# Attention: the products with the values segment by segment, both parities of heads in turn

## The chip, the cores and the metric

The kernel runs on one core of one Trainium2 chip. A core has a matrix engine (TensorE: PE in the profile, its weight loads PEld), VectorE (DVE), ScalarE (ACT), GpSimd (POOL) and SyncE (SP), which issues the transfers here. The metric is the device time of one execution in microseconds (us).

## The reference

One inference step of a two-layer streaming encoder over 1024 new frames of one stream and 64 frames of a running one, width 1024, all in float32. Layer 0 is RWKV-7 time mixing and a SwiGLU feed-forward; layer 1 is sliding-window attention over keys and values that are shared, with a learned sink per head, and another feed-forward. The part that matters here is the attention: 16 query heads of 64, four key/value heads, chunks of 64 frames; the queries of a chunk see the keys of their own chunk and of the two before it.

```python
s = jnp.einsum('bnqhgd,bnkhd->bnhgqk', qc, kb, preferred_element_type=jnp.float32) * ATTN_SCALE
s = jnp.where(valid[None, :, None, None, None, :], s, NEG_INF)
p = sink_softmax(s, sinks)              # exp(s - m) / (sum exp(s - m) + exp(sink - m))
o = jnp.einsum('bnhgqk,bnkhd->bnqhgd', p.astype(v.dtype), vb)
```

## The kernel before, in words

Activations are held with features on the partitions. The tokens are worked in two halves: A, 512 frames, and B, the other 512 and the 64 of the running stream. The dense products (line names `dp`, L433 to L435) take three matmuls for each product, of float32 values split into a high and a low part: each streams 288 columns (half B) or 512 (half A) through a full 128x128 array.

`attend` calls `chunk` 8 times for half A and 9 times for half B, so 17 chunks. A chunk is worked in two passes `m`, each with four key/value-and-group combinations in two parities `par`: heads of parity 0 lie on partitions 0 to 63 and of parity 1 on 64 to 127. One pass is, in the order of the code:

1. the scores `sc`, one matmul for each `g` and `par` (L1259): keys on 64 partitions, 64 to 192 columns;
2. maximum, exponential and sum on VectorE and ScalarE, and the scaling by the reciprocal (L1261 to L1284);
3. for each parity, transposes `pt` of the probabilities (L1290), two for each segment of keys, and a copy of each segment to `a_PT` in SBUF (L1291), the first segment's on ScalarE, the second's on VectorE;
4. the products with the values `po` (L1294): for parity 0 into partitions 0 to 63 of one PSUM tile, for parity 1 into 64 to 127, one matmul for each segment, the segments added up in PSUM;
5. one copy of the 128x256 tile into the query's place `a_q` (L1297, ScalarE).

A window of keys lies in one or two tiles of 128 values. The first two chunks have one segment (of 64 or 128 keys), the other 15 have two: 128 and 64, or, where the window begins in the middle of a tile, 128 and 128, with zeros ahead. So there are 34 passes and 128 products with the values; 30 of the passes have two segments.

Buffers: `sc` has two PSUM tiles, `pt` two, `po` one; the probabilities `a_P` and their transposes `a_PT` have two each.

What stands on each engine is not the order of the code: the framework's scheduler places instructions by priority (`prio(6)` and `prio(9)` for the two attention passes over half A and half B) and by its own timing of the engines. The feed-forward of the other half has the next priority after the attention (`prio(7)`: half B, layer 0; `prio(10)`: half A, layer 1), and its `dp` matmuls are filled in wherever the attention is not ready on TensorE. Each engine then runs its own list strictly in order.

Of the kernel before, what the change touches and what calls it, by code (L numbers as in the profile page):

```python
# [1137 lines left out]
class Attention:  # L1138
# [95 lines left out]
    def chunk(self, half, i, q):  # L1234
        nc, dn, c = self.nc, self.dn, self.c
        V, S, G = nc.vector, nc.scalar, nc.gpsimd
        ch = i if half == "A" else 8 + i


        if ch == 16:  # L1240
            key = lambda h, m: self.kS[h, m, :]
            pad, nk, seg = 0, 192, [(0, 128, self.vC), (128, 64, self.vS)]
        else:
            k0, k1 = max(0, ch - 2) * 64, ch * 64 + 64
            key = lambda h, m: self.kT[h, m, k0:k1]
            pad, nk = k0 % 128, k1 - k0
            seg = [(at - k0 + pad, min(128, k1 - at), self.v[:, at // 128, :]) for at in range(k0 - pad, k1, 128)]
        sinks = self.vec["sinks"]
        for m in range(2):
            sc = []  # L1250
            mx = self.t([128, 6, 4], "mx", 2)
            for par in range(2):
                self.n += 1
                p = self.ps.tile([128, 512], F32, name=f"sc_{self.n}", tag="rc", bufs=2)[:, :2 * nk].rearrange("p (a k) -> p a k", a=2)
                sc.append(p)
            for g in range(2):
                for par in range(2):
                    h = slice(par * 64, par * 64 + 64)
                    nc.tensor.matmul(sc[par][:, g, :], lhsT=q[h, i, 4 * m + 2 * g:4 * m + 2 * g + 2, :].rearrange("p a t -> p (a t)"), rhs=key(h, m), start=True, stop=True)  # L1259
            for par in range(2):  # L1260
                V.tensor_reduce(out=mx[:, 0, 2 * par:2 * par + 2], in_=sc[par], axis=AX.X, op=ALU.max)  # L1261
            sk = sinks[:, 4 * m:4 * m + 4]
            V.scalar_tensor_tensor(out=mx[:, 1, :], in0=mx[:, 0, :], scalar=SCALE, in1=sk, op0=ALU.mult, op1=ALU.max)
            V.tensor_scalar(out=mx[:, 2, :], in0=mx[:, 1, :], scalar1=-1.0, scalar2=None, op0=ALU.mult)
            V.tensor_tensor(out=mx[:, 3, :], in0=sk, in1=mx[:, 1, :], op=ALU.subtract)
            S.activation(mx[:, 3, :], mx[:, 3, :], AF.Exp)
            P = []
            for par in range(2):
                e = self.t([128, 2, 256], "P", 2)
                if pad:  # L1270
                    G.memset(e[:, :, 0:pad], 0.0)
                for g in range(2):
                    x = 2 * par + g
                    S.activation(e[:, g, pad:pad + nk], sc[par][:, g, :], AF.Exp, scale=SCALE, bias=mx[:, 2, x:x + 1], accum_out=mx[:, 4, x:x + 1])
                P.append(e)
            V.tensor_tensor(out=mx[:, 5, :], in0=mx[:, 4, :], in1=mx[:, 3, :], op=ALU.add)
            V.reciprocal(out=mx[:, 5, :], in_=mx[:, 5, :])
            self.n += 1
            po = self.ps.tile([128, 512], F32, name=f"po_{self.n}", tag="ry", bufs=1)[:, :256]
            for par in range(2):  # L1280
                e = P[par]
                for g in range(2):
                    x = 2 * par + g
                    V.tensor_scalar(out=e[:, g, pad:pad + nk], in0=e[:, g, pad:pad + nk], scalar1=mx[:, 5, x:x + 1], scalar2=None, op0=ALU.mult)  # L1284
                self.n += 1
                pt = self.ps.tile([128, 512], F32, name=f"pt_{self.n}", tag="rp", bufs=2).rearrange("p (s g q) -> p s g q", s=2, g=2)
                eT = self.t([128, 2, 2, 128], "PT", 2)
                for si, (at, n, vv) in enumerate(seg):
                    for g in range(2):
                        nc.tensor.transpose(pt[0:n, si, g, :], e[:, g, at:at + n], c["id"])  # L1290
                    (S.copy if si == 0 else V.tensor_copy)(eT[0:n, si], pt[0:n, si])  # L1291
                for si, (at, n, vv) in enumerate(seg):
                    col = (2 * m + par) * 64
                    nc.tensor.matmul(po[par * 64:par * 64 + 64, :], lhsT=vv[0:n, col:col + 64],  # L1294
                                     rhs=eT[0:n, si].rearrange("p g q -> p (g q)"),
                                     start=si == 0, stop=si == len(seg) - 1)
            S.copy(q[:, i, 4 * m:4 * m + 4, :], po.rearrange("p (i t) -> p i t", i=4))  # L1297
# [126 lines left out]
```

## Time and profile before

| | |
|---|---|
| median of 3 runs | 3066.93 us (3064.41 to 3069.12) |
| profiled execution | 3068.17 us, its span 3066.4 us |
| PE busy | 2881.6 us, 94% of the span |
| DVE, ACT, POOL busy | 62%, 45%, 30% |
| granted TensorE clock, mean | 0.960 |
| attention over half A | about 1456 to 1640 us of the span |
| attention over half B | about 2099 to 2360 us of the span |

In the views below each row of the timeline gives the start in us from the span's beginning, how long the row's instructions took from the first start to the last end, the engine, the line, the operation, what it writes and reads, the part of the array (rows by columns) and the shape, and how many records the row holds. A float32 matmul with `sc` or `po` leaves two records, a transpose and a `dp` matmul one. The ends of matmuls overlap with the next one's start, so the time that a row occupies TensorE is read from its start to the next row's start.

### The profile page before, as it was taken

To read this page: it belongs to the slowest core of one execution; us is meant where nothing else is said; L and a number is where in the kernel's file an instruction comes from. 1 tells how busy PE (TensorE), PEld (TensorE's weight loads), DVE (VectorE), ACT (ScalarE), POOL (GpSimd) and SP (SyncE) were. 2 spreads that over 40 slices of the span, in tenths; PEclk is the share of its full clock that TensorE was granted. 3 is DMA by queue.
4 is the path that set the end of the run, shared out by engine and by line. 5 is a ranking of instruction groups with operands and counts; after the bars stand their busy time and mean duration, and the time that the engine had idled before them with its cause. 6 is when DMAs were issued, how large, how long until landed. Compare 5 with 4: busy or idle time off the path is not lost. (4 is left out here: it accounts for less than half of the span.)

```text
span 3066.4 us, 51529 instructions
## 1 busy us (share of the span) xinstructions
PE 2881.6 (94%) x19650; PEld 2475.1 (81%) x19650; DVE 1899.9 (62%) x3964; ACT 1371.4 (45%) x2489; POOL 915.9 (30%) x785
## 2 busy tenths in 40 slices
PE   6898888987999989999999999999999999999998
PEld 5677777876777767887789999887667889899998
DVE  8887798968998993357553333665555334633334
ACT  7766665544445542244653222344553233322222
POOL 6455123323343332224211222243111222322221
PEclk9999789989899999999999999999999999999999
DMA  4645353353232225232112222222112332322222
GB/s 144 174 119 149 109 140 102 109 130 118 77 97 87 90 70 139 93 111 86 62 42 73 83 83 83 77 82 79 59 62 67 95 96 73 110 83 83 84 82 70
DMA packets 262047, 289.10 MB, mean 94 GB/s; under 512 B 125028, under 2 KB 143972, under 8 KB 261800
## 3 DMA queue, kind: packets, MB, share of 16 engines
q1 hardware_dynamic: 261800, 285.81, 31.3%
q8 instruction: 154, 2.52, 0.4%
q14 instruction: 93, 0.76, 0.1%
HBM read 243.18 MB, written 41.16 MB: 93 GB/s over the span
## 5 line engine op out<-in xcount | busy, mean ns | idle before, releaser
L433 PE MATMUL dp<-xh,wh 128*128 128x288 f32 (+2 forms) x3480 | 1181.1, 341 | 26.1 <-DVE hx L962 10.2
L434 PE MATMUL dp<-xl,wh 128*128 128x288 f32 (+2 forms) x3480 | 1175.5, 338 | 10.6 <-POOL xl L426 6.3
L435 PE MATMUL dp<-xh,wl 128*128 128x288 f32 (+2 forms) x3480 | 1172.4, 337 | 0.0
L393 ACT CAST wh<-wr 128x512 fp32r<-128x512 f32 x730 | 446.2, 619 | 823.6 <-PE dp L434 633.0
L433 PEld LDWEIGHTS dp<-xh,wh 128*128 128x128 f32 x3480 | 667.0, 192 | 100.4 <-DVE hx L962 14.7
L434 PEld LDWEIGHTS dp<-xl,wh 128*128 128x128 f32 x3480 | 668.5, 192 | 73.3 <-POOL xl L426 7.6
L435 PEld LDWEIGHTS dp<-xh,wl 128*128 128x128 f32 x3480 | 668.7, 192 | 62.0 <-issue 6.2
L394 POOL TENSOR_TENSOR wl<-wr,wh 128x512 fp32r<-128x512 f32 x243 | 339.2, 1396 | 1059.0 <-ACT wh L393 954.0
L394 DVE TENSOR_TENSOR wl<-wr,wh 128x512 fp32r<-128x512 f32 x487 | 376.3, 776 | 431.5 <-ACT wh L393 423.0
L433 PE MATMUL dp<-mh,wh 128*128 128x288 f32 (+1 forms) x808 | 254.5, 315 | 1.2 <-DVE a_xB L962 1.0
L435 PE MATMUL dp<-mh,wl 128*128 128x288 f32 (+1 forms) x808 | 254.1, 314 | 0.0
L434 PE MATMUL dp<-ml,wh 128*128 128x288 f32 (+1 forms) x808 | 253.5, 314 | 0.0
L943 DVE TENSOR_TENSOR st<-st,dp 128x288 f32<-128x288 f32 (+1 forms) x132 | 70.0, 530 | 229.0 <-PE dp L435 228.6
L962 DVE TENSOR_TENSOR a_xB<-dp,a_xB 128x288 f32<-128x288 f32 x352 | 158.1, 455 | 82.9 <-PE dp L435 82.7
L945 POOL TENSOR_TENSOR xl<-st,xh 128x288 fp32r<-128x288 f32 (+1 forms) x102 | 101.8, 998 | 330.4 <-ACT xh L944 321.6
L433 PEld LDWEIGHTS dp<-mh,wh 128*128 128x128 f32 x808 | 152.3, 189 | 10.8 <-issue 2.4
L435 PEld LDWEIGHTS dp<-mh,wl 128*128 128x128 f32 x808 | 152.3, 188 | 8.1 <-issue 1.8
L434 PEld LDWEIGHTS dp<-ml,wh 128*128 128x128 f32 x808 | 152.4, 189 | 6.6 <-issue 0.8
L190 ACT COPY r_f<-r_G 32x1024 f32<-32x1024 f32 x68 | 136.0, 1999 | 37.1 <-DVE r_f L226 25.0
L962 DVE TENSOR_TENSOR hx<-dp,hx 128x512 f32<-128x512 f32 x176 | 119.5, 684 | 44.9 <-PE dp L435 44.4
L215 DVE TENSOR_TENSOR r_f<-r_f,r_f 128x60 f32<-128x60 f32 (+5 forms) x476 | 119.2, 281 | 0.5
L944 ACT CAST xh<-st 128x288 fp32r<-128x288 f32 (+1 forms) x102 | 50.2, 492 | 136.2 <-DVE st L943 135.1
(343 smaller groups left out, 3889.3 us busy)
## 6 DMA issues: line engine op xcount, KB each, us to landing
wr<-in_ffn_in SPq DMA_DIRECT2D x352, 256.0 KB
wr<-in_ffn_out SPq DMA_DIRECT2D x176, 256.0 KB
wr<-in_rkv SPq DMA_DIRECT2D x90, 256.0 KB
wr<-in_rwo SPq DMA_DIRECT2D x32, 256.0 KB
wr<-in_wq SPq DMA_DIRECT2D x32, 256.0 KB
wr<-in_wo SPq DMA_DIRECT2D x32, 256.0 KB
r_r_s<-s_s SPq DMA_DIRECT2D x17, 256.0 KB
r_sv<-s_vt SPq DMA_DIRECT2D x17, 256.0 KB
```

The costliest lines, as they stand in the source:

```text
L190: S.copy(st[32 * q:32 * q + 32].rearrange("p (t g j) -> p t g j", g=4, j=8), src)
L215: V.tensor_tensor(out=Z[:, h, 1:3, r0:4, 0:j], in0=Z[:, h, a, r0:4, j:j + 2].rearrange("p r c -> p c r").unsqueeze(3).broadcast_to([128, 2 ...
L393: nc.scalar.copy(h, x)
L394: (nc.gpsimd if self.turn % 3 == 0 else nc.vector).tensor_tensor(out=l, in0=x, in1=h, op=ALU.subtract)
L433: self.nc.tensor.matmul(ps, lhsT=wh, rhs=xh, start=i == 0, stop=False)
L434: self.nc.tensor.matmul(ps, lhsT=wh, rhs=xl, start=False, stop=False)
L435: self.nc.tensor.matmul(ps, lhsT=wl, rhs=xh, start=False, stop=i == last)
L943: V.tensor_tensor(out=t[o], in0=t[o], in1=p, op=ALU.mult)
L944: S.copy(a.hi[:, q], t[o])
L945: G.tensor_tensor(out=a.lo[:, q], in0=t[o], in1=a.hi[:, q], op=ALU.subtract)
L962: V.tensor_tensor(out=self.x[m][:, q], in0=p, in1=self.x[m][:, q], op=ALU.add)
```

## The change

The products with the values of a pass are taken out of the loop over the parities. The loop now makes the transposes and copies of both parities and keeps the two `a_PT` tiles in a list; then a loop over the segments multiplies, for each segment, parity 0 and parity 1 one after the other. The matmuls, their operands and their number are the same, and so are the copies, the buffers and the sums: each half of the tile still adds its first and then its second segment.

```diff
             po = self.ps.tile([128, 512], F32, name=f"po_{self.n}", tag="ry", bufs=1)[:, :256]
+            eTs = []
             for par in range(2):
                 e = P[par]
...
                     (S.copy if si == 0 else V.tensor_copy)(eT[0:n, si], pt[0:n, si])
-                for si, (at, n, vv) in enumerate(seg):
+                eTs.append(eT)
+
+            for si, (at, n, vv) in enumerate(seg):
+                for par, eT in enumerate(eTs):
                     col = (2 * m + par) * 64
                     nc.tensor.matmul(po[par * 64:par * 64 + 64, :], lhsT=vv[0:n, col:col + 64],
```

The scheduler makes new lists from it. The lines of `chunk` behind the change are one to four higher: L1290 becomes L1291, L1291 L1292, L1294 L1298. On TensorE, in a pass over half A with two segments of 128 keys (`pt` the transposes of one parity, `po` the products with the values, `sc` the scores of a later pass, `dp` the feed-forward; rows with - are before, with + now):

```order
 L434 MATMUL dp_16455<-ml_14887,wh_16443 128x288
 L435 MATMUL dp_16455<-mh_14886,wl_16444 128x288
-L1290 MATMUL pt_15481<-c_id,a_P_15468 128x128 x2
-L1294 MATMUL po_15478<-a_PT_15482,vtok 64x256
-L1290 MATMUL pt_15493<-c_id,a_P_15472 128x128 x2
+L1291 MATMUL pt_15481<-c_id,a_P_15468 128x128 x2
+L1291 MATMUL pt_15491<-c_id,a_P_15472 128x128 x2
+L1298 MATMUL po_15478<-a_PT_15482,vtok 64x256
+L1298 MATMUL po_15478<-a_PT_15492,vtok 64x256
 L433 MATMUL dp_16455<-xh_14938,wh_16449 128x288
```

The product of parity 0's first segment stood between the transposes of the two parities; now the transposes are together, and behind them the first segment's products of both parities. Some 20 `dp` matmuls later, in the same pass:

```order
 L434 MATMUL dp_16482<-ml_14783,wh_16443 128x288
 L435 MATMUL dp_16482<-mh_14782,wl_16444 128x288
-L1294 MATMUL po_15478<-a_PT_15482,vtok 64x256
-L1294 MATMUL po_15478<-a_PT_15494,vtok 64x256
+L1298 MATMUL po_15478<-a_PT_15482,vtok 64x256
+L1298 MATMUL po_15478<-a_PT_15492,vtok 64x256
 L1259 MATMUL sc_15554<-kT,a_q_14575 128x192 x2
-L1294 MATMUL po_15478<-a_PT_15494,vtok 64x256
 L433 MATMUL dp_16482<-mh_14834,wh_16443 128x288
```

The third product of this stretch, parity 1's second segment, stood alone behind two score matmuls; now the second segments of the two parities stand together and nothing of `po` is behind the scores. On VectorE, in a pass over half B (`a_PT` the copies of the second segments, `hx` the feed-forward's sums out of PSUM, `a_mx` the softmax sums):

```order
 L394 TENSOR_TENSOR wl_23085<-wr_23086,wh_23084 128x512
 L962 TENSOR_TENSOR hx_10480<-dp_22991,hx_10480 128x512
-L1291 COPY a_PT_22020<-pt_22019 128x256
 L394 TENSOR_TENSOR wl_23091<-wr_23092,wh_23090 128x512
-L1291 COPY a_PT_22032<-pt_22031 128x256
+L962 TENSOR_TENSOR hx_10487<-dp_23011,hx_10487 128x512
+L1292 COPY a_PT_22020<-pt_22019 128x256
+L1292 COPY a_PT_22030<-pt_22029 128x256
 L1276 TENSOR_TENSOR a_mx_22042<-a_mx_22042 128x4
-L962 TENSOR_TENSOR hx_10487<-dp_23011,hx_10487 128x512
 L1277 RECIPROCAL a_mx_22042<-a_mx_22042 128x4
```

Here both copies have moved behind one more of the feed-forward's sums, which waits for a `dp` tile of TensorE. In half A the order on VectorE is the same as before but for one stretch of a few rows; in half B the copies and sums change places in this way at several passes. SyncE's list is the same.

## The prediction

> **What bounds the kernel now.** I read the page's busy shares first, then the busy time by stage, then who waited on TensorE, then single stretches of TensorE's timeline. The page, and the stages from the attention over half A to the end (length, then the busy us of each engine, the clock and the transfers' share):
>
> ```profile
> PE 2881.6 (94%) x19650; PEld 2475.1 (81%) x19650; DVE 1899.9 (62%) x3964; ACT 1371.4 (45%) x2489; POOL 915.9 (30%) x785
> 1455.00:1640.00 185.00, 180.48 (x1140) 146.58 (x1139) 98.91 (x278) 102.01 (x275) 32.85 (x39) 0.99 0.17 52
> 1640.00:2099.00 459.00, 448.68 (x3185) 435.38 (x3184) 220.96 (x354) 148.40 (x279) 127.19 (x103) 0.99 0.27 83
> 2099.00:2360.00 261.00, 257.94 (x1154) 177.34 (x1153) 142.38 (x325) 130.00 (x322) 46.71 (x49) 0.99 0.20 63
> 2360.00:3066.00 706.00, 689.20 (x4468) 643.49 (x4466) 298.41 (x531) 212.92 (x389) 163.88 (x138) 0.99 0.28 86
> ```
>
> The first and third stages are the two attention passes. TensorE is busy for 180.5 of 185.0 us and 257.9 of 261.0 there, and for 98% of what follows; no other engine reaches 56%, the transfers 28%. For whom TensorE waits between 1450 and 2360 us:
>
> ```profile
> PE dp L1193 <- ACT st L1213: 5.4, 1, 5.4
> PE sc L1259 <- ACT a_P L1274: 3.4, 2, 2.1
> PE dp L433 <- DVE a_xB L962: 3.4, 3, 2.0
> ```
>
> Of the attention's own lines only two score matmuls wait, 3.4 us together, and no product `po` and no transpose does. The waiting is on the other side, as in the stage of half A:
>
> ```profile
> ACT a_q L1297 <- PE po L1294: 26.1, 12, 4.2
> DVE a_mx L1261 <- PE sc L1259: 18.6, 18, 2.1
> DVE a_PT L1291 <- PE pt L1290: 10.3, 13, 2.5
> ```
>
> ScalarE and VectorE wait for TensorE. So what TensorE's list costs in these two stages is what they cost, and time taken out of it moves everything behind it forward, as long as TensorE stays the bound.
>
> **What a product costs, alone and beside its partner.** The busy time of 94% hides that the 128x64 and 64x64 pieces leave half of the array or more unused. Three stretches show what can share it:
>
> ```profile
> 1477.34 0.29 PE L433 MATMUL dp<-xh,wh 128*128 128x288 f32 x1
> 1477.56 0.65 PE L1294 MATMUL po<-a_PT,vtok 64*64 64x256 f32 x4
> 1478.14 0.40 PE L434 MATMUL dp<-xl,wh 128*128 128x288 f32 x1
> 1478.38 0.29 PE L435 MATMUL dp<-xh,wl 128*128 128x288 f32 x1
> 1478.51 0.29 PE L433 MATMUL dp<-xh,wh 128*128 128x288 f32 x1
> ...
> 1499.59 0.65 PE L1294 MATMUL po<-a_PT,vtok 128*64 128x256 f32 x2
> 1500.17 0.40 PE L433 MATMUL dp<-xh,wh 128*128 128x288 f32 x1
> ...
> 2330.07 1.08 PE L1294 MATMUL po<-a_PT,vtok 128*64 128x256 f32 x6
> 2331.09 0.91 PE L1259 MATMUL sc<-kS,a_q 64*128 64x192 f32 x4
> ```
>
> A product leaves two records. At 1499.59 one product stands alone: 0.58 us until the next start. At 1477.56, in a chunk of one segment, four records, the products of both parities one behind the other: also 0.58 us. Two neighbours in different column halves run at once. At 2330.07 three products of 128 rows in the order parity 0, 1, 1 take 1.02 us: the first two at once, the third 0.44 behind them. But equal shapes are needed, as a stretch of half B shows:
>
> ```profile
> 2127.93 1.22 PE L1294 MATMUL po<-a_PT,vtok 64*64 64x256 f32 x4
> 2129.08 0.59 PE L1259 MATMUL sc<-kT,a_q 64*128 64x192 f32 x2
> 2129.60 0.64 PE L1294 MATMUL po<-a_PT,vtok 64*64 64x256 f32 x2
> 2130.18 0.60 PE L1259 MATMUL sc<-kT,a_q 64*128 64x192 f32 x4
> 2130.70 0.66 PE L1290 MATMUL pt<-c_id,a_P 128*128 128x128 f32 x4
> ```
>
> At 2127.93 parity 0's second segment (64 rows) and parity 1's first (128 rows) stand together in different halves, and take 1.15 us: no overlap. A lone 64-row product takes 0.58 (2129.60 to 2130.18).
>
> The Trainium skill says both things in "TensorEngine Tiling (Array Packing)", section Tiling Modes: tiles operate independently, and a change of the tiling mode, not of the tile alone, drains the engine; the trace agrees, with 0.58 against 1.15 us.
>
> **The sum.** *Products.* I counted neighbours in TensorE's list. Before, 91 of the 128 products stand without a partner of their shape, 11 pairs run at once, and 5 triples are like the one at 2330.07: 91 x 0.58 + 11 x 0.58 + 5 x 1.02 = 64.3 us. After, 38 stand alone (where the scheduler put a transpose, a score or a `dp` between) and 45 pairs are formed: 38 x 0.58 + 45 x 0.58 = 48.1 us. **-16.2 us.** Each pair kind, of 128 and of 64 rows, has run before, so I give this term no bounds of its own.
>
> By "TensorE: Matmul & The Clock Gate" of the Trainium skill (Part 3, Measured speedup vs the span model) three column tiles gained 2.38, not 3; an estimate from that makes a pair about 0.73 us, and with 29 pairs more than before the term would be some 4 us smaller. No run here shows such a loss: the pair takes 0.58.
>
> *Scores.* They change places too, since the products no longer stand between them. Their two parities lie in different row halves:
>
> ```profile
> 1502.07 0.91 PE L1259 MATMUL sc<-kT,a_q 64*128 64x192 f32 x4
> 1502.91 0.40 PE L434 MATMUL dp<-xl,wh 128*128 128x288 f32 x1
> ...
> 2099.90 0.92 PE L1259 MATMUL sc<-kT,a_q 64*128 64x192 f32 x8
> 2100.75 0.50 PE L433 MATMUL dp<-xh,wh 128*128 128x512 f32 x1
> ```
>
> Two of one parity take 0.84 us, four in turn 0.85; from the stretch above, one alone takes 0.52 (2129.08) and two of different parity 0.52 (2130.18). Of the 120 with 192 columns, before: 24 alone, 36 twos of one parity, 10 mixed twos, one four in turn: 12.5 + 30.2 + 5.2 + 0.9 = 48.8 us. After: 14 alone, 24 twos, 3 mixed twos, 4 fours in turn make 7.3 + 20.2 + 1.6 + 3.4 = 32.5; besides there are 8 threes and 3 fours with the parities as 0, 0, 1, 1, which the trace doesn't have. A three costs between 0.84 and 1.36 (0.84 + 0.52), a four between 0.85 and 1.68. I take 0.9 and 1.27, by the triple of products, where only what has no partner was added: 7.2 + 3.8. **-5.3 us**, between -7.0 and -0.4.
>
> *Changes of shape.* The first `dp` behind a narrow group takes 0.24 us instead of 0.13 (1478.14 to 1478.38, then to 1478.51), the last one ahead 0.22 (1477.34 to 1477.56). Returns from `po` or `sc` to `dp` go from 61 to 82: 21 x 0.11 = 2.3. Entries from `dp` go from 65 to 62: -0.3. The rest is in the transposes:
>
> ```profile
> 1531.30 0.38 PE L1290 MATMUL pt<-c_id,a_P 128*128 128x128 f32 x2
> 1531.61 0.65 PE L1294 MATMUL po<-a_PT,vtok 128*64 128x256 f32 x2
> 1532.18 0.44 PE L1290 MATMUL pt<-c_id,a_P 128*128 128x128 f32 x2
> 1532.38 0.38 PE L433 MATMUL dp<-xh,wh 128*128 128x288 f32 x1
> 1532.59 0.29 PE L434 MATMUL dp<-xl,wh 128*128 128x288 f32 x1
> ```
>
> Two of them ahead of a product take 0.31; ahead of `dp` 0.20 and 0.08 more in the `dp` itself. Transposes followed by a narrow product or score go from 39 to 47, those that follow a product from 29 to 9; that is less than 1 us either way. **+2 us**, between 0 and +4.
>
> *New waits.* The second segment's product of parity 1 now comes with parity 0's, ahead of the scores, and needs VectorE's second copy sooner. In the pass above:
>
> ```profile
> 1531.87 0.41 DVE L1291 COPY a_PT<-pt 128x256 f32<-128x256 f32 x1
> 1532.72 0.42 DVE L1291 COPY a_PT<-pt 128x256 f32<-128x256 f32 x1 [0.44 <-ACT a_P L1274]
> ...
> 1534.95 0.65 PE L1294 MATMUL po<-a_PT,vtok 128*64 128x256 f32 x4
> 1535.53 0.92 PE L1259 MATMUL sc<-kT,a_q 64*128 64x192 f32 x4
> 1536.38 0.65 PE L1294 MATMUL po<-a_PT,vtok 128*64 128x256 f32 x2
> ```
>
> The copy ends at 1533.14, the product that read it last started at 1536.38; even at the pair's place, 1534.95, it has 1.8 us to spare. Behind that product wait the scores and all of `dp`, so a late copy would cost its full lateness. The first segment's products now stand behind parity 1's transposes instead of ahead of them, but those were the next instruction on TensorE anyway. The copies that moved behind a `hx` sum on VectorE wait for a `dp` tile that TensorE's new list finishes ahead of these transposes. I take 0; the upper bound is as much again as the attention waits for now, 3.4 us. No transfer moves, and TensorE's list outside the two stages is the same.
>
> Together -16.2 - 5.3 + 2 = -19.5 us. The profiled execution took 3068.17 us (span 3066.4): 3048.7. It was 1.24 us above the median of the runs, 3066.93; on that footing **3047.5 us**. With the terms' bounds the gain is 23.2 to 9.2 us: 3043.7 to 3057.7.
>
> **Rivals.** *The pairs don't overlap* where a wait stands on the second one, so the change doesn't do what it says. Then the products cost as before, and the scores and shapes leave -3.3: 3063.6, no change that can be told. Against it: at 1477.56 the second product has its own copy to wait for, and ran beside the first all the same.
>
> *Part of the gain is handed back*: with TensorE faster in the attention, softmax and copies become the bound there. ScalarE's 102.0 of 185.0 and VectorE's 98.9 leave room on average, but both work in order. At half the gain, 3057. For it: the scores' 3.4 us of waits for ScalarE's exponentials; against it, the 26.1 us for which ScalarE waits for `po`.
>
> *Slower*: VectorE's second copy gets stuck. Its place is the pair of second segments, 30 passes. If it slips behind one more sum whose `dp` tile comes 24 matmuls of 0.13 us later (3.1 us), less the 1.8 to spare, each pass waits 1.3 us: 30 x 1.3 = 39, less 19.5, gives 3086.5. It decides from 19.5 / 30 = 0.65 us beyond the slack on. Against it: no `po` waits now, VectorE's order in half A hardly changes, and where half B's does, the tile is done in time.
>
> **Chances.** My forecast with its bounds 0.77, a gain beyond them 0.04, part handed back 0.11, pairs without overlap 0.05, slower 0.03. Below about 0.2% (6.1 us) no change can be told. Faster by more takes the first two, and nearly all of the third: 0.91; the same 0.06; slower 0.03. I set the range to 3041 to 3060: the forecast's own, a little more gain than the terms allow, and most of what is handed back.
>
> **What would show it.** Right: rows of `po` with four records that last 0.58 us to the next start, in both 128-row and 64-row chunks; the two attention stages shorter by some 19 us together, the stages behind them as long as before; TensorE still waiting for nothing of `a_PT`. Wrong: TensorE waits on `po` with VectorE or ScalarE as the releaser, four-record rows of 1.15 us, or the stage of half A or B as long as before at a higher idle time of TensorE.

## The result and the profile after

The changed kernel takes 3042.66 us (median of 4 runs, 3041.14 to 3053.0) against 3065.67 us (4 runs): a ratio of 0.9931, 95% interval 0.9907 to 0.9955. Timed once more, it took 3047.31 us (5 runs) against 3065.88 (9 runs): 0.9936, 0.9922 to 0.9949. So the change makes the kernel 0.6 to 0.7% faster, some 20 us. 3047.5 us was forecast.

The page of the changed kernel, and the same stages as before, cut at the same times:

```profile
PE 2854.4 (94%) x19650; PEld 2463.5 (81%) x19650; DVE 1885.7 (62%) x3964; ACT 1371.7 (45%) x2491; POOL 920.5 (30%) x785
1455.00:1640.00 185.00, 180.49 (x1171) 149.51 (x1168) 98.16 (x277) 102.92 (x279) 33.06 (x39) 0.99 0.17 55
1640.00:2099.00 459.00, 448.52 (x3178) 433.32 (x3176) 224.66 (x359) 149.74 (x282) 129.78 (x104) 1.00 0.27 83
2099.00:2360.00 261.00, 258.06 (x1219) 185.45 (x1220) 133.62 (x333) 134.24 (x329) 48.60 (x52) 0.99 0.22 69
2360.00:3040.00 680.00, 664.28 (x4365) 623.84 (x4363) 288.99 (x517) 206.59 (x379) 159.77 (x134) 0.99 0.28 87
```

TensorE is as busy as before in the two attention stages, but gets more done: 1171 instead of 1140 records in the first 185 us, 1219 instead of 1154 in the 261 us of the third row. Whom TensorE waits for between 1450 and 2360 us:

```profile
PE dp L1193 <- ACT st L1213: 5.4, 1, 5.4
PE sc L1259 <- ACT a_P L1274: 3.4, 2, 2.1
PE dp L433 <- DVE a_xB L962: 3.4, 3, 2.0
```

These are the same three rows as before, to the tenth. No wait on `po` or on a copy was added. And the pairs, in TensorE's timeline, of 64 and of 128 rows:

```profile
1555.51 0.65 PE L1298 MATMUL po<-a_PT,vtok 64*64 64x256 f32 x4
1556.09 0.91 PE L1259 MATMUL sc<-kT,a_q 64*128 64x192 f32 x4
...
1552.35 0.65 PE L1298 MATMUL po<-a_PT,vtok 128*64 128x256 f32 x4
1552.93 0.40 PE L434 MATMUL dp<-xl,wh 128*128 128x288 f32 x1
```

Four records, two products, 0.58 us to the next start, in both shapes. Where the scheduler left something between the partners, each still pays for itself:

```profile
1529.77 0.65 PE L1298 MATMUL po<-a_PT,vtok 128*64 128x256 f32 x2
1530.35 0.44 PE L1291 MATMUL pt<-c_id,a_P 128*128 128x128 f32 x2
1530.72 0.65 PE L1298 MATMUL po<-a_PT,vtok 128*64 128x256 f32 x2
1531.29 0.40 PE L433 MATMUL dp<-xh,wh 128*128 128x288 f32 x1
```

To compare the terms I added up, for each kernel, the times from each start on TensorE to the next, by what had started, from the first score to one late `dp` matmul, the 15,307th matmul record of every kernel; the lists of all the kernels are the same ahead of this stretch and behind it. Waits of the engine, its idle time ahead of a matmul, are taken out of the sums and stand apart. The experiments named in the table follow in the next section. All in us, from one profiled execution each:

| kernel | products | scores | transposes | `dp` | waits | together |
|---|---|---|---|---|---|---|
| before | 63.8 | 53.5 | 27.2 | 769.9 | 17.9 | 932.3 |
| the change | 48.0 | 46.5 | 29.3 | 768.5 | 17.9 | 910.2 |
| the change, again | 48.0 | 46.5 | 29.6 | 769.9 | 17.9 | 911.9 |
| parity by parity | 63.1 | 49.5 | 28.7 | 767.7 | 17.9 | 927.0 |
| crossed turns | 62.4 | 45.9 | 27.3 | 769.8 | 18.1 | 923.6 |
| second segment first | 44.8 | 48.8 | 23.8 | 770.9 | 19.1 | 907.4 |
| exponentials in turn | 46.9 | 43.1 | 29.7 | 767.7 | 18.0 | 905.5 |
| transposes first | 47.5 | 46.1 | 25.9 | 770.8 | 18.1 | 908.4 |
| second first, exponentials in turn | 44.2 | 41.9 | 24.3 | 769.2 | 19.1 | 898.8 |

Of the span's 25.8 us less (3066.4 to 3040.6), 22.1 lie in this stretch; the other 3.7 lie ahead of it and behind it, where TensorE's two lists are equal. The start of the first score shows how far executions spread. From the view of the line of the scores, before, the change, the change again, and the next section's first experiment (duration min, median and max in ns, then first and last start):

```profile
L1259 PE MATMUL sc<-kT,a_q x256: 272/323/529, 1456.2 to 2306.8; 64*128 64x192 f32 x112, 64*128 64x64 f32 x8, 64*128 64x128 f32 x8
L1259 PE MATMUL sc<-kT,a_q x256: 272/323/600, 1454.5 to 2288.0; 64*128 64x192 f32 x112, 64*128 64x64 f32 x8, 64*128 64x128 f32 x8
L1259 PE MATMUL sc<-kT,a_q x256: 272/323/629, 1449.3 to 2284.5; 64*128 64x192 f32 x112, 64*128 64x64 f32 x8, 64*128 64x128 f32 x8
L1259 PE MATMUL sc<-kT,a_q x256: 272/323/547, 1460.2 to 2308.8; 64*128 64x192 f32 x112, 64*128 64x64 f32 x8, 64*128 64x128 f32 x8
```

The first score starts at 1449.3 to 1460.2 us, behind the same work; the two profiles of the change alone are 5.2 us apart. This is why the medians of a few runs differ by some us, and why the stretch is the better measure of a term.

### The profile page after: what moved, and what is told of

Same layout as the page of the kernel before. It is cut to its first block, busy times and chain, and to the rows that moved or that the text cites. A ratio compares the mean times of both kernels' runs of the same rounds, so it can differ in the third digit from the quotient of the medians.

```text
span 3040.6 us, 51529 instructions
## 1 busy us (share of the span) xinstructions
PE 2854.4 (94%) x19650; PEld 2463.5 (81%) x19650; DVE 1885.7 (62%) x3964; ACT 1371.7 (45%) x2491; POOL 920.5 (30%) x785
## 5 line engine op out<-in xcount | busy, mean ns | idle before, releaser
L433 PE MATMUL dp<-xh,wh 128*128 128x288 f32 (+2 forms) x3480 | 1180.3, 340 | 29.2 <-DVE hx L962 11.4
```

Source lines behind the costliest of these rows:

```text
L433: self.nc.tensor.matmul(ps, lhsT=wh, rhs=xh, start=i == 0, stop=False)
```

## The experiments

**Parity by parity.** The theory: neighbours of one shape in two halves of the array run at once, and the turn of the parities makes them neighbours. A rival: what pays is that the products went behind both transposes. This kernel does the second alone.

```diff
-            for si, (at, n, vv) in enumerate(seg):
-                for par, eT in enumerate(eTs):
+            for par, eT in enumerate(eTs):
+                for si, (at, n, vv) in enumerate(seg):
```

> Half of the change alone: the transposes of both parities come first, as changed, but the products go parity by parity again (parity 0's segments, then parity 1's). Counted in TensorE's list, products without a partner of their shape are 86 (38 with the change, 91 before), pairs at once 6, triples 10. Theory (equal shapes in two column halves run at once): the products cost 86 x 0.58 + 6 x 0.58 + 10 x 1.02 = 63.6 us, the scores some 3 us more than with the change; about 17 us of the gain is gone, 3060 us, within 8 us of the kernel before. Rival (moving the products behind both transposes is what pays, by fewer changes of shape and earlier release of the probabilities): the returns to the feed-forward are 75 against 82, so the gain of 23 us stays, 3043 us.

3062.41 us against 3063.56 (10 and 17 runs), ratio 0.9990, 0.9977 to 1.0003. The products are back at 63.1 us. In half A, in TensorE's timeline, parity 0's second segment and both of parity 1's stand together, neighbours in different halves but not of one shape:

```profile
1560.18 1.79 PE L1298 MATMUL po<-a_PT,vtok 64*64 64x256 f32 x6
1561.90 0.91 PE L1259 MATMUL sc<-kT,a_q 64*128 64x192 f32 x4
```

Three products, 1.72 us: three times 0.57. The rival falls for the products. The scores keep 4.0 of their 7.0 us (49.5 against 53.5): that part comes with the new place and not with the turn.

**Crossed turns.** This keeps the place, but lets the parities go 0, 1, 1, 0, so that neighbours in different halves always belong to different segments. Where the segments have 128 and 64 keys, such neighbours differ in shape; where both have 128, they don't.

```diff
-            for si, (at, n, vv) in enumerate(seg):
-                for par, eT in enumerate(eTs):
+            turns = [(0, 0), (1, 1), (0, 1), (1, 0)] if len(seg) == 2 else [(0, 0), (0, 1)]
+            begun = set()
+            for si, par in turns:
...
-                                     start=si == 0, stop=si == len(seg) - 1)
+                                     start=par not in begun, stop=len(seg) == 1 or par in begun)
```

> The products are in the place of the change, but the turns are crossed: parity 0 segment 0, parity 1 segment 1, parity 0... as (segment, parity) = (0,0), (1,1), (0,1), (1,0). In the 16 passes with segments of 128 and 64 keys no two neighbours have the same shape in different halves; in the 14 passes of 128 and 128 they have. Changes of shape between attention and feed-forward are fewer than with the change (72 returns against 82). Theory (pairs): the 32 products of 64 rows and the 32 of 128 in those passes stand alone at 0.57 us, 62.5 us for all products against 48.0, less 1 for the scores and 1 for the returns: about 12 us slower than the change, 3055 us. Rival (the place and the fewer shape changes pay): 3041 us or less.

3055.48 against 3063.56 us (8 and 17 runs), ratio 0.9970, 0.9952 to 0.9988: some 10 us slower than the change by the ratios (0.9970 against 0.9936), 13 by the stretch (923.6 against 910.2). In TensorE's timeline, the last three products of a pass with segments of 128 and 64, then of one of 128 and 128 (the first product, of parity 0, stands alone ahead of them):

```profile
1553.58 1.79 PE L1301 MATMUL po<-a_PT,vtok 64*64 64x256 f32 x6
1555.30 0.92 PE L1259 MATMUL sc<-kT,a_q 64*128 64x192 f32 x4
...
1532.27 1.08 PE L1301 MATMUL po<-a_PT,vtok 128*64 128x256 f32 x6
1533.28 0.59 PE L1259 MATMUL sc<-kT,a_q 64*128 64x192 f32 x2
```

Both rows are three products of parity 1, 1 and 0. The first are of 64, 128 and 64 rows and take 1.72 us, the second all of 128 rows and take 1.01. The order of the halves is the same, and only the rows of the products differ: it is the equal shape that the pairs need, not the turn as such.

**Exponentials in turn.** To test the scores' term by itself: what changes is when ScalarE lets the two score tiles go.

```diff
                 if pad:
                     G.memset(e[:, :, 0:pad], 0.0)
-                for g in range(2):
+                P.append(e)
+            for g in range(2):
+                for par in range(2):
                     x = 2 * par + g
-                    S.activation(e[:, g, pad:pad + nk], sc[par][:, g, :], AF.Exp, scale=SCALE, bias=mx[:, 2, x:x + 1], accum_out=mx[:, 4, x:x + 1])
-                P.append(e)
+                    S.activation(P[par][:, g, pad:pad + nk], sc[par][:, g, :], AF.Exp, scale=SCALE, bias=mx[:, 2, x:x + 1], accum_out=mx[:, 4, x:x + 1])
```

> The change, and the exponentials on ScalarE also go with the two parities in turn, so that the two score tiles come free closer together and more of the score matmuls stand together. Theory (the score matmuls of the two row halves run at once as well, whatever their order, when they stand together): scores about 2 us less by the count of the groups, returns to the feed-forward 72 against 82 (1.1 us less), products 1 us less: about 5 us faster than the change, 3038 us. Rival (the scores' part of the gain was chance): as the change, 3043 us.

3039.75 against 3063.56 us (4 and 17 runs), ratio 0.9913, 0.9888 to 0.9938. The scores take 43.1 us instead of 46.5 and the products 46.9 instead of 48.0, with the same waits: 4.7 us less in the stretch, 5 expected. The interval overlaps with the change's; the stretch is what carries the verdict, one execution of it. What the scores gain from is in the changed kernel already, in TensorE's timeline:

```profile
2186.55 0.93 PE L1259 MATMUL sc<-kT,a_q 64*128 64x192 f32 x8
2187.40 0.66 PE L1291 MATMUL pt<-c_id,a_P 128*128 128x128 f32 x4
...
2135.51 0.92 PE L1259 MATMUL sc<-kT,a_q 64*128 64x192 f32 x6
2136.35 0.44 PE L1291 MATMUL pt<-c_id,a_P 128*128 128x128 f32 x2
```

At 2186.55 four scores stand in the list as parity 0, 0, 1, 1 and take 0.85 us, as long as four in turn (0.85 before, at 2099.90) and as two of one parity alone (0.84). At 2135.51 three take 0.84. So within such a group the two row halves each work off their own row of matmuls, and the longer one sets the time.

**Second segment first.** If shapes should change seldom, all four products of a pass should stand together. The second segment's pair waits longest, for VectorE's copies; put first, it takes the other along.

```diff
-            for si, (at, n, vv) in enumerate(seg):
+            for si, (at, n, vv) in reversed(list(enumerate(seg))):
...
-                                     start=si == 0, stop=si == len(seg) - 1)
+                                     start=si == len(seg) - 1, stop=si == 0)
```

> The change with the segments in the reverse order: the second segment's pair, which waits for VectorE's copies, goes first, and the first segment's pair right behind it, so that all four products stand together instead of at two places of the pass. Counted: products 44.6 us instead of 48.0, returns to the feed-forward 61 against 82 (2.3 us less), transposes followed by a narrow product or score 14 against 47 (3 us less), scores 1.5 us more: about 6 us faster than the change, 3036 us. Rival (the first pair's later place holds the copies' buffers longer and TensorE waits for ScalarE or VectorE): no gain or a loss against the change, 3043 us or more, with waits of TensorE on the attention's lines over the 3.4 us of now.

3041.33 against 3063.56 us (4 and 17 runs), ratio 0.9915, 0.9894 to 0.9936. The stretch is 2.8 us shorter than the change's, less than half of what was expected: products 3.2 and transposes 5.5 us less, but scores 2.3 more, 1.2 more of waits, and `dp` 2.4 more. Against the change's second profile it is 4.5 us. The transposes end ahead of `dp` more often, and 83 `dp` matmuls instead of 55 stand right behind a transpose: these cost 2.5 us more, so that the transposes' own 5.5 us are worth 3.0, as was expected of them. The rival's waits did not come: those on the attention's lines stay at 3.4 us, and what is longer is a wait of `dp` for VectorE (2.3 us instead of 1.3).

In 15 of the 30 passes with two segments the four products stand together, in the others three of them. In TensorE's timeline in half B, of 128 and 128 keys, then of 128 and 64:

```profile
2147.65 1.08 PE L1298 MATMUL po<-a_PT,vtok 128*64 128x256 f32 x8
2148.66 0.60 PE L1259 MATMUL sc<-kT,a_q 64*128 64x192 f32 x4
...
2136.09 1.23 PE L1298 MATMUL po<-a_PT,vtok 64*64 64x256 f32 x8
2137.25 0.43 PE L1259 MATMUL sc<-kT,a_q 64*128 64x192 f32 x2
```

Four products of one shape take 1.01 us, less than two pairs (2 x 0.58). Where the shape changes between the pairs, the four take 1.16 us: standing together then saves nothing in the products.

**Transposes first.** The transposes of the second segment wait for the copy of the first out of the same PSUM tile, and come some 20 `dp` matmuls later. Here both copies come behind both transposes.

```diff
                 for si, (at, n, vv) in enumerate(seg):
                     for g in range(2):
                         nc.tensor.transpose(pt[0:n, si, g, :], e[:, g, at:at + n], c["id"])
+                for si, (at, n, vv) in enumerate(seg):
                     (S.copy if si == 0 else V.tensor_copy)(eT[0:n, si], pt[0:n, si])
```

> The change, and in each parity the transposes of both segments come ahead of both copies, so that the second segment's transposes no longer wait for the first one's copy out of the same tile. Counted: products 47.4 us (48.0), no transposes right ahead of a narrow group (47 with the change, 4 us less), entries from the feed-forward into narrow groups 89 against 62 (2.4 us more): 2 us less than the change, 3041 us. Rival (TensorE had its place in the pass from the wait on the copy, and now runs into the softmax): waits on transposes or scores over the 3.4 us of now, 3045 us or more.

3040.93 against 3065.88 us (4 and 9 runs), ratio 0.9918, 0.9904 to 0.9931, and 1.8 us less than the change in the stretch: the transposes 3.4 us less, `dp` 2.3 more. The waits on the attention's lines stay at 3.4 us, so the rival falls; that the gain over the change is real is not shown, since it is within what the stretch varies by (910.2 and 911.9 for the change itself).

**Both gains together.** The reverse segments and the exponentials in turn.

> The reverse order of the segments and the exponentials in turn, together, on the changed kernel. By the count of the groups: products 44 us (48.0 with the change), scores 3.6 us less than with the change, returns to the feed-forward 55 against 82 (3 us less), transposes ahead of a narrow group 14 against 47 (3 us less), some of it taken back by longer transposes' ends: about 10 us less than the change between the first score and the last product, 3033 us. Rival (the two gains are of the same waits and do not add up): 3040 us, as either alone.

3034.62 against 3065.88 us (4 and 9 runs), ratio 0.9898, 0.9884 to 0.9911: the fastest, about 12 us ahead of the change by the ratios (0.9936 to 0.9898). Products 44.2, scores 41.9, transposes 24.3 us, 898.8 together, 11.4 us less than the change (10 expected; 13.1 against its second profile). Alone, the two edits took 2.8 and 4.7 us off. They add up, and the rest is in the scores: the reverse order alone made them 2.3 us longer and the exponentials in turn 3.4 shorter, and both together make them 4.6 shorter, since scores that the reverse order had driven apart stand together again (eight fours of 192 columns instead of two).

**The change again.** No edit.

> The changed kernel itself, beside the others and the kernel before on one chip, for a narrower interval. Theory: 22 us between the first score and the last product, so 0.993 of the time before; the 3 to 4 us more that the first profile showed ahead of and behind the attention, where nothing is changed, are the spread between executions, and are not there on average. Rival (they are a part of the change's effect): 0.9915 or less.

0.9936, 0.9922 to 0.9949: the theory's side. The stretch is 911.9 us, the products and scores as in the first profile to a tenth.

## Why the prediction was right, point by point

*The bound.* Right: TensorE waits for the same three rows as before, and what came out of its list came off the end (22.1 us in the stretch, 25.8 of the span).

*Products, -16.2 us.* 63.8 to 48.0: -15.8, both times. The pairs take 0.58 us, and the count of partners in the list was all that the sum needed. All the 45 pairs ran at that price. By an estimate from the Trainium skill, "TensorE: Matmul & The Clock Gate" (Part 3, Measured speedup vs the span model: three column tiles gained 2.38, not 3), some 4 us of this were to be lost; the measurement, 0.58 us for a pair as for one alone, decides against such a loss for two column halves.

*Scores, -5.3 us.* -7.0, at the end of the bounds. The step that was mis-sized is the price of the groups that the trace before did not have: for three and for four as 0, 0, 1, 1 I took 0.9 and 1.27, reasoning that only what has no partner beside it adds time. The runs show 0.84 and 0.85 (2135.51 and 2186.55 above), so the 8 threes and 3 fours come to 9.3 us and not 11.0, which is the 1.7 us that the term is off by. A matmul need not stand beside its partner, only in the same group of one shape.

*Changes of shape, +2 us.* +1.4 us in the first profile of the change and +2.1 in the second. The rows of the table don't show this, since `dp` came to 1.4 us less and then to the same, and the transposes to 2.1 and 2.4 us more. The parts show when the `dp` matmuls are sorted by what stands beside them and only their time above the usual is added up (0.132 us for 288 columns, 0.232 for 512). Right behind a product or a score this was 7.6 us before and is 9.8 now, both times: +2.2, where the prediction had 2.3. Right behind a transpose it was 7.3 us (81 matmuls) and is 4.9 and 5.0 (55), so the transposes together with the `dp` behind them came to 0.3 us less and 0.2 more, within the "less than 1 us either way". The entries, `dp` right ahead of a product or a score, came to 0.5 and 0.3 us less, where the prediction had 0.3. All other `dp` matmuls together differ by -0.7 and +0.3 us, with no change in them.

*New waits, 0.* Right; neither VectorE's second copies nor the `hx` sums ahead of them held TensorE.

Together -19.5 forecast, -22.1 and -20.4 in the stretch; the first pair of medians differs by 23.0, the second by 18.6. These two differ by more than the two stretches do; what the rest of the kernel spreads by is enough for that (5.2 us for the first score's start above). The gain of 23.0 is just within the terms' 9.2 to 23.2; the time itself, 3042.66, lies 1.0 below their lower end of 3043.7, because the kernel before was 1.3 us faster in these runs than the 3066.93 that was reckoned from. That the second median, 3047.31, meets the 3047.5 to 0.2 us is chance, since two medians of the changed kernel lie 4.7 us apart.

*The rivals.* No pair failed to overlap: all 45 took 0.58 us. Nothing was handed back, and the copy never got stuck: TensorE's waits in the stretch are 17.9 us before and now.

## What to carry to other kernels

Where TensorE is the bound, look at the shapes of neighbours in its list and not only at how busy it is: matmuls that use half of the rows or half of the columns ran at the price of one when a partner of the same shape in the other half stood in the same group, and at full price when one of another shape did. The loop order in the source decides which partners the scheduler can put together; count them in the list that it makes, and price each group by rows of the trace. Then gather the groups: fewer changes of shape, by putting the part that waits longest first, and buffers that come free together, gave another 11 to 13 us in the stretch here. What a shape change costs is in the row of the neighbour as well: sort those rows by what stands beside them before you call such a term too small to be seen.

## What the runs showed of the hardware that was not expected

Within a group of one shape the two halves of the array ran through their own matmuls independently of how they alternate in the list: four scores as 0, 0, 1, 1 took 0.85 us, four in turn 0.85, two of one half alone 0.84. One half behind the other would have taken 1.68 us by these figures, and with only direct neighbours at once the prediction's estimate was 1.27. For products of 128 rows, three took 1.01 us, in the order 0, 1, 1 as in 1, 1, 0, and four 1.01. In the order 1, 1, 0 (the crossed turns at 1532.27) the second record starts 13 ns behind the first, where one product alone starts its second record 267 ns later: the product of parity 0, last of the three in the list, runs beside the first. So in these groups TensorE kept to its list within each half of the array, but not across the two, and the words ahead of the prediction, that each engine runs its list strictly in order, are too strong for it.
